# Second MLP product of a hybrid encoder layer: a step of the weight split done by adding or casting DMAs

## Chip, cores and metric

The kernel runs on one core of a Trainium2 chip. The metric is the device time of one execution in microseconds (us).

## What is computed

One layer of a bidirectional encoder on 256 tokens of width 2048 in float32: input projection, attention, a gated linear recurrence, a merge, an MLP, a per-layer embedding and a last norm. The part that the change touches is the second product of the MLP, whose weight `w_down` has 8192 rows and 2048 columns:

```python
h = rmsnorm(x, g_mlp[i])
u = jnp.square(jax.nn.relu(jnp.einsum('bsd,df->bsf', h, w_up[i])))
x = x + jnp.einsum('bsf,fd->bsd', u, w_down[i])
```

## The kernel before

All weights are streamed from HBM once, in chunks of 1 MB: a tile `raw` of 128 partitions by 2048 float32. `load` (L101 to L106) issues one DMA for a chunk on SyncE's queue. The matrix products run in the 32-bit format float32r, whose mantissa is shorter than float32's, and the lost precision is brought back by splitting each operand in two: `hi` is the value rounded to float32r, `lo` the rest. `prep_half` (L108 to L116) does this for half a chunk, 128x1024: ScalarE copies `raw` into a `hi` tile (L112, the copy rounds), VectorE writes `lo` = `raw` - `hi` (L113). `raw` has 3 buffers, `hi` and `lo` have 4 halves each, which is two chunks.

A product is then the sum of three: `x_hi w_hi + x_lo w_hi + x_hi w_lo`. In `gemm_mov` (the second MLP product among others) one chunk holds four blocks of the contraction for 512 columns. TensorE runs 16 matmuls that read the chunk's `hi` halves and then 8 that read its `lo` halves (L196), each 128x512. Blocks 0 and 1 lie in the first half of the chunk, blocks 2 and 3 in the second:

```python
for a, ws in ((0, w[0]), (1, w[0]), (0, w[1])):
    for kk in range(4):
        for t in ts:
            last_mm[0] = pe.matmul(ps[t], xs(X, k)[:, a, t * P:(t + 1) * P], wsl(ws, kk, 512), ...)
```

The order of the chunks is written out in a list at the start (`order`, `plan`). The MLP's steps are u0 u1 d0 u2 d1 u3 d2 d3: a step u computes a quarter of the 8192 hidden features with `w_up` (16 chunks), a step d, here called a pass, multiplies that quarter by `w_down` (16 chunks: four groups j of 512 output columns with four chunks c each), keyed `("dn", 4 * pass + j, c)`. At the end of each group VectorE adds the two accumulators to the residual (L674).

When TensorE's code comes to chunk i, `next_w` (L123 to L132) has issued the loads up to chunk i + 2 and the split of chunk i + 1. A tile framework puts the semaphores: a load waits until the reader of the `raw` buffer's earlier chunk is done, a `hi` or `lo` write until TensorE has read that buffer's earlier half, two chunks back. Each engine, GpSimd (POOL) and SyncE's queue (SP) too, takes its instructions strictly in its own order. POOL computes small things (L300 and others) and issues no DMA.

Of the kernel before, what the change touches and what calls it, by code (L numbers as in the profile page):

```python
# [7 lines left out]
AF = mybir.ActivationFunctionType  # L8
ALU = mybir.AluOpType
AX = mybir.AxisListType  # L10
PSUM = bass.MemoryType.PSUM

P = 128
D = 2048
S = 256
# [11 lines left out]
def build(tc, xT, xtok, pT, gains, gfin_in, ropet, ident_in, masks_in, ghg_in, lb_in,  # L27
          w_mov, w_st, w_oa, w_oh, w_out, w_up, w_dn, w_pg, w_ple, out):
    nc = tc.nc
    act, dve, pool, pe, sp = nc.scalar, nc.vector, nc.gpsimd, nc.tensor, nc.sync  # L30
# [5 lines left out]
    order = []  # L36
# [18 lines left out]
    for step in MLP:  # L55
        c = int(step[1])
# [6 lines left out]
    for j in range(4):  # L63
        plan("pg", 4, j)
    aps = {"in": w_mov, "st": w_st, "oa": w_oa, "oh": w_oh, "out": w_out, "up": w_up, "dn": w_dn, "pg": w_pg,
           "ple": w_ple}

    import contextlib
    with contextlib.ExitStack() as es:
# [14 lines left out]
        def nm(s):  # L84
            cnt[0] += 1
            return f"{s}_{cnt[0]}"
# [7 lines left out]
        def mps():  # L94
            return psm.tile([P, 512], F32, tag="m", name=nm("m"))

# [1 line left out]
        raws, preps = {}, {}  # L98
        pos = [0, 0, 0]

# [7 lines left out]
        def prep_half(i, hf):  # L108
            sl = raws[i][:, hf * 1024:(hf + 1) * 1024]
            hi = wraw.tile([P, 1024], F32R, tag="hi", bufs=4, name=nm("hi"))  # L110
            lo = wraw.tile([P, 1024], F32R, tag="lo", bufs=4, name=nm("lo"))
            act.activation(hi, sl, AF.Copy)  # L112
            dve.tensor_tensor(lo, sl, hi, ALU.subtract)  # L113
            his, los = preps.setdefault(i, ([], []))
            his.append(hi)
            los.append(lo)  # L116
# [14 lines left out]
            pos[0] += 1  # L131
            return preps.pop(i)  # L132

# [1 line left out]
        clock = [0.0]  # L135
        last_mm = [None]
        woven = []
# [24 lines left out]
            o = (k % per) * n  # L162
            return t[:, o:o + n]

        # act tensors are pairs of [P, 8, 2, 256] (hi | lo)
        def xs(X, k):
            return X[k // 8][:, k % 8]

        def gemm_st(key, X, last=None):
            """[128 e, hi-lo x S] in PSUM; `last` runs before the last quarter of the contraction is read."""  # L170
            his, los = next_w(key)
            ps = gps()
            for k in range(KT):
                if k == 12 and last:
                    last()
                x = xs(X, k)
                pe.matmul(ps, wsl(his, k, P), x, start=k == 0, stop=False)  # L177
                pe.matmul(ps[:, :S], wsl(los, k, P), x[:, 0, :], start=False, stop=k == KT - 1)  # L178
                tick(0.327)
            return ps  # L180
# [4 lines left out]
            return z  # L185

        def gemm_mov(arr, j, X, last=None, stagger=False):
            """[128 tokens, 512 e] in PSUM for both token tiles; staggered, the first one ends well before the second."""
            ps = [gps() for _ in range(NT)]

            def chunk(c, w, ts):
                for a, ws in ((0, w[0]), (1, w[0]), (0, w[1])):
                    for kk in range(4):
                        k = 4 * c + kk
                        for t in ts:
                            last_mm[0] = pe.matmul(ps[t], xs(X, k)[:, a, t * P:(t + 1) * P], wsl(ws, kk, 512),  # L196
                                                   start=k == 0 and a == 0 and ws is w[0],
                                                   stop=k == KT - 1 and ws is w[1])
                        tick(0.216 * len(ts))

            for c in range(2 if stagger else 4):
                if c == 3 and last:
                    last()
                chunk(c, next_w((arr, j, c)), range(NT))
            if stagger:
                if last:
                    last()
                ws = [next_w((arr, j, c)) for c in (2, 3)]
                for t in range(NT):
                    for c in (2, 3):  # L210
                        chunk(c, ws[c - 2], (t,))
            return ps
# [2 lines left out]
            return gemm_mov("in", GROUPS.index(g), X)  # L215

        def to_T(srcs, X, e0, gain=None):
            """four [tokens, 128] blocks of both token tiles, transposed, scaled and split into X[e0:e0 + 4]."""
            yield 2.5
            for e in (e0, e0 + 2):  # L220
                tp = mps()
                for a in range(2):
                    for t in range(NT):
                        o = (e - e0 + a) * P
                        pe.transpose(tp[:, a * S + t * P:a * S + (t + 1) * P], srcs[t][:, o:o + P], ident)  # L225
                if gain is None:
                    dst = X[e // 8][:, e % 8:e % 8 + 2]
                    tv = tp.rearrange("p (e t) -> p e t", e=2)
                    act.activation(dst[:, :, 0, :], tv, AF.Copy)
                    dve.tensor_tensor(dst[:, :, 1, :], tv, dst[:, :, 0, :], ALU.subtract)  # L230
                else:
                    for a in range(2):
                        dst, tv, g = xs(X, e + a), tp[:, a * S:(a + 1) * S], gain[:, e + a:e + a + 1]
                        act.activation(dst[:, 0, :], tv, AF.Copy, scale=g)
                        dve.scalar_tensor_tensor(dst[:, 1, :], tv, g, dst[:, 0, :], ALU.mult, ALU.subtract)  # L235
                yield 0.5
# [2 lines left out]
            n = nm("c")  # L239
            return cst.tile(shape, dt, tag=n, name=n)  # L240

# [1 line left out]
        ph1, st1 = open_pool("ph1", side="right")  # L243

        def t1(shape, tag, bufs=1, dt=F32):
# [14 lines left out]
        quarter = lambda X, qd: X[qd // 2][:, 4 * (qd % 2):4 * (qd % 2) + 4]  # L260
# [39 lines left out]
            pool.tensor_tensor(outt, v, nhalf[:, :n], ALU.pow)  # L300

        def bcast_r(rt, R):
            """R [P, S] = rt laid along the free axis on every partition."""
            ps = mps()
            for t in range(NT):
                pe.matmul(ps[:, t * P:(t + 1) * P], rt[:, t:t + 1].to_broadcast([P, P]), ident,
                          start=True, stop=True)
            dve.tensor_copy(R, ps[:, :S])
# [14 lines left out]
        def setup():  # L323
# [12 lines left out]
            dve.tensor_scalar(rtok, rtok, 1.0 / D, EPS, ALU.mult, ALU.add)  # L336
            rsq(rtok, rtok, NT)
            dve.tensor_scalar(rtok_s, rtok, HD ** -0.5, None, ALU.mult)
            # rope tables with the gains folded in: [q|k][cos|sin]
            for w in (1, 0):  # L340
                for t in range(NT):
                    for a in range(2):
# [7 lines left out]
            for qd in range(4):  # L350
# [1 line left out]
                pool.tensor_tensor(xq, xq, R0.unsqueeze(1).to_broadcast([P, 4, S]), ALU.mult)  # L352
                split(Hm, xq, qd)
                yield 3.0
            # hgrn lower bounds: softmax over the two layers, entry 0
            dve.tensor_tensor(lmx, lbt[:, 0], lbt[:, 1], ALU.max)
            dve.tensor_tensor(lex, lbt, lmx.unsqueeze(1).to_broadcast([P, 2, 2, KT]), ALU.subtract)
            act.activation(lex, lex, AF.Exp)
# [2 lines left out]
            dve.tensor_tensor(low, lex[:, 0], lsum, ALU.mult)  # L361
            dve.tensor_tensor(oml, lex[:, 1], lsum, ALU.mult)

# [1 line left out]
        def heads_T(ps, w, tag, pause):  # L365
            """per-head rmsnorm, gain, rope, then transpose into [P(d), 4, hi-lo, S]."""
            zas = []
            for t in range(NT):
                ss = t1([P, 4], "ss", 2)
                scr = t1([P, HD], "scr", 2)  # L370
                for h in range(4):
                    act.activation(scr, ps[t][:, h * HD:(h + 1) * HD], AF.Square,
                                   scale=rtok_s[:, t:t + 1], accum_out=ss[:, h:h + 1])
# [18 lines left out]
            for t in range(NT):  # L392
# [4 lines left out]
                hi, lo = (dstT[:, :, a, t * P:(t + 1) * P] for a in range(2))  # L397
# [76 lines left out]
        flush()  # L474
        st1.close()

# [1 line left out]
        ph2, st2 = open_pool("ph2", side="right")  # L478

        def t2(shape, tag, bufs=2, dt=F32):  # L480
# [4 lines left out]
        def scan_head(h, q, T, vi, gg):  # L485
# [8 lines left out]
            tiles = lambda ap: ap[:, :S].rearrange("p (t s) -> p t s", t=NT)  # L494
# [11 lines left out]
            for li, L in enumerate(LEVELS):  # L506
# [14 lines left out]
                if L < 64:  # L521
# [3 lines left out]
                    T = Tn  # L525
# [5 lines left out]
                    dve.copy_predicated(SD, masks[:, 0].unsqueeze(1).to_broadcast([P, NT, P]), tiles(pd))  # L531
                yield {1: 3.5, 64: 2.6}.get(L, 2.0)
            px = mps()
            # column block t of SX: S^T[s in the other tile, t]
            pe.matmul(px[:, P:2 * P], KK[:, 0, 0:P], QQ[:, 1, P:2 * P], start=True, stop=True)
            pe.matmul(px[:, 0:P], KK[:, 1, P:2 * P], QQ[:, 0, 0:P], start=True, stop=True)
            SX = t2([P, NT, P], "SX", 1)
# [25 lines left out]
        for j in range(4):  # L563
# [11 lines left out]
            for h in range(4 * j, 4 * j + 4):  # L575
                ps = gemm_st(("st", 3 * h), Hm)
                q = t2([P, S], "q")
# [4 lines left out]
                T = t2([P, 2, S], "T1")  # L582
# [4 lines left out]
                    dve.tensor_scalar(T[:, d], T[:, d], oml[:, d, h:h + 1], low[:, d, h:h + 1], ALU.mult, ALU.add)  # L587
                weave(scan_head(h, q, T, vi, gg))

# [1 line left out]
        ctok = lambda tag: [com.tile([P, 512], F32, tag=tag, bufs=2, name=nm(tag)) for _ in range(NT)]  # L591
        MX = None
        for j in range(4):
# [18 lines left out]
                dve.tensor_tensor(ya[t], ya[t], yb[t], ALU.add)  # L612
            weave(to_T(ya, MX, 4 * j))

# [1 line left out]
        xr = bigt(F32, [P, NT, D])  # L616
        for t in range(NT):
            sp.dma_start(xr[:, t], xtok[t])
# [3 lines left out]
        rr = [ctile([P, NT]) for _ in range(3)]  # L622
# [2 lines left out]
            act.activation(junk(), rows(j)[t], AF.Square, accum_out=sums[i][:, t, j:j + 1])  # L625

        def row_r(i, ts=slice(0, NT)):
            """rr[i] = rsqrt(mean square + eps) per token."""
            r = rr[i][:, ts]
            dve.tensor_reduce(r, sums[i][:, ts], AX.X, ALU.add)  # L630
            dve.tensor_scalar(r, r, 1.0 / D, EPS, ALU.mult, ALU.add)  # L631
            rsq(r, r, ts.stop - ts.start)
# [6 lines left out]
                squares(0, j, t)  # L639
            weave(to_T(rows(j), H1, 4 * j, gn[:, 1]))  # L640

# [1 line left out]
        UA = UB = Hp = t4 = None  # L643
        r1s = ctile([P, NT])
        for step in MLP:
            c = int(step[1])
# [30 lines left out]
                if c == 3:  # L677
                    weave(to_T(rows(j), Hp, 4 * j, gn[:, 2]))

# [1 line left out]
        pH = bigt(F32R, [P, 2, 2, S])  # L681
        pf = com.tile([P, 2, S], F32, tag="ya", bufs=2, name=nm("pf"))
        gfin = bigt(F32, [P, D])
# [42 lines left out]


def _stationary(w, n):
    """[2048, 128 n] -> [n, 128 p, 16 k * 128 e]."""
    return np.ascontiguousarray(w.reshape(KT, P, n, P).transpose(2, 1, 0, 3).reshape(n, P, D))  # L730


def _moving(w):
    """[2048, 512 n] -> [n, 4 c, 128 p, 4 k * 512]."""
    return np.ascontiguousarray(w.reshape(4, 4, P, -1, 512).transpose(3, 0, 2, 1, 4).reshape(-1, 4, P, D))


def _feat(v):
    """[..., 2048] -> [128 p, ..., 16 k]."""
    return np.moveaxis(v.reshape(v.shape[:-1] + (KT, P)), -1, 0)  # L740


# [73 lines left out]
```

## Time and profile of the kernel before

| | us |
|---|---|
| median of 2 runs | 1992.3 |
| lowest and highest run | 1992.04, 1992.57 |
| profiled execution, span from first to last instruction | 1992.7 |
| TensorE matmul busy in that span | 1967.5 |
| VectorE busy | 1238.1 |
| ScalarE busy | 947.6 |
| GpSimd busy | 144.0 |

The profile is of one execution, read by the hardware profiler; the page gives its span and no other time for it, and this span is 0.4 us longer than the median of the timed runs. A row of the timeline begins with its start and its length in us. `x16` behind a row is the count of instructions that were merged into it. PE is TensorE, DVE VectorE, ACT ScalarE, SPq SyncE's DMA queue. A matmul's length counts its way through the array, so matmuls overlap, and the distance of starts is what one costs.

### The profile page before, as it was taken

How to read it: one execution, taken by the hardware profiler on the slowest of the kernel's cores; microseconds unless marked ns; L12 is line 12 of the kernel's file. 1: busy time of each engine (PE TensorE's matmuls, PEld its weight loads, DVE VectorE, ACT ScalarE, POOL GpSimd, SP SyncE). 2: the span in 40 equal slices, each digit the busy share in tenths (PEclk: the TensorE clock that was granted, in tenths of full speed). 3: DMA queues.
4: the chain of work that ended last, by engine and by line, in shares of the span. 5: the costliest groups of instructions: out<-in, count | busy, mean ns of one | idle time of the engine just before them, and what ended most of it. 6: DMA issues, size and time to landing. Idle time of an engine off the chain costs nothing.

```text
span 1992.7 us, 25647 instructions
## 1 busy us (share of the span) xinstructions
PE 1967.5 (99%) x9948; PEld 1664.1 (84%) x9948; DVE 1238.1 (62%) x1722; ACT 947.6 (48%) x1495; POOL 144.0 (7%) x175
## 2 busy tenths in 40 slices
PE   8999999999999999999999999999999999999998
PEld 6788888888888888888888888888888888888886
DVE  6877687686785874545545566665565456545555
ACT  5576555454554553444443454443344344434543
POOL 2300030120220210000000000000000000000001
PEclk9999999999999999999999999999999999999999
DMA  8444444544434435555565555555555555555553
GB/s 324 167 145 148 148 149 148 175 142 166 166 136 168 167 138 183 189 194 186 192 240 192 183 175 186 189 190 190 190 190 190 190 185 189 197 190 181 201 193 123
DMA packets 51673, 358.56 MB, mean 180 GB/s; under 512 B 5984, under 2 KB 6240, under 8 KB 9056
## 3 DMA queue, kind: packets, MB, share of 16 engines
q1 hardware_dynamic: 51552, 356.93, 50.7%
q8 instruction: 78, 1.28, 0.2%
q14 instruction: 43, 0.35, 0.0%
HBM read 354.81 MB, written 2.10 MB: 179 GB/s over the span
## 4 chain that ended last, share of the span: by engine, by line
PE 96%; DVE 2%; issue 1%; DMA 1%; ACT 0%; POOL 0%; SPq 0%; POOLq 0%; DVEq 0%; ACTq 0%
PE g L196 58%; PE g L177 20%; PE g L178 10%; PE m L509 3%; PE m L443 1%; PE m L423 1%; PE g L696 1%; DMA big<-xT 1%; DVE lo L113 1%; PE m L225 1%; PE m L544 0%; PE m L529 0%; PE m L543 0%; PE m L454 0%; ACT hi L112 0%
## 5 line engine op out<-in xcount | busy, mean ns | idle before, releaser
L113 DVE TENSOR_TENSOR lo<-raw,hi 128x1024 fp32r<-128x1024 f32 x660 | 810.2, 1246 | 649.4 <-ACT hi L112 593.0
L112 ACT ACTIVATE hi<-raw 128x1024 fp32r<-128x1024 f32 x660 | 679.0, 1055 | 807.0 <-PE g L196 488.6
L196 PE MATMUL g<-hi,big 128*128 128x512 f32 x2688 | 658.8, 394 | 9.0 <-ACT hi L112 9.0
L177 PE MATMUL g<-big,hi 128*128 128x512 f32 x1792 | 643.9, 402 | 0.0
L196 PEld LDWEIGHTS g<-hi,big 128*128 128x128 f32 x2688 | 501.8, 189 | 111.2 <-ACT hi L112 10.3
L178 PE MATMUL g<-big,lo 128*128 128x256 f32 x1792 | 503.3, 281 | 0.0
L177 PEld LDWEIGHTS g<-big,hi 128*128 128x128 f32 x1792 | 337.3, 188 | 76.5 <-DVE big L235 0.3
L196 PE MATMUL g<-lo,big 128*128 128x512 f32 x1344 | 344.2, 394 | 0.0
L178 PEld LDWEIGHTS g<-big,lo 128*128 128x128 f32 x1792 | 340.0, 190 | 0.4
L196 PEld LDWEIGHTS g<-lo,big 128*128 128x128 f32 x1344 | 249.3, 189 | 49.0
L196 PE MATMUL g<-hi,UB 128*128 128x512 f32 x512 | 125.1, 396 | 0.0
L196 PEld LDWEIGHTS g<-hi,UB 128*128 128x128 f32 x512 | 96.2, 188 | 22.4
L300 POOL TENSOR_TENSOR c<-c,c 128x2 f32<-128x2 f32 (+1 forms) x5 | 3.2, 640 | 1164.2 <-DVE c L631 1150.5
L509 PE MATMUL m<-QQ,kc 128*128 128x128 f32 x448 | 72.8, 286 | 2.8 <-ACT kc L501 2.6
L509 PEld LDWEIGHTS m<-QQ,kc 128*128 128x128 f32 x448 | 64.1, 191 | 11.5 <-ACT kc L501 5.3
L501 ACT ACTIVATE kc<-KK 128x256 f32<-128x256 f32 x112 | 47.7, 436 | 50.8 <-PE m L509 25.9
L523 POOL TENSOR_TENSOR T<-T 128x256 f32<-128x256 f32 (+2 forms) x96 | 54.0, 563 | 202.6 <-DVE T L587 186.7
L196 PE MATMUL g<-lo,UB 128*128 128x512 f32 x256 | 65.5, 396 | 0.0
L196 PE MATMUL g<-hi,MX 128*128 128x512 f32 x256 | 63.3, 397 | 0.0
L516 DVE TENSOR_TENSOR QQ<-QQ,T 128x256 f32<-128x256 f32 x112 | 52.2, 466 | 13.0 <-PE m L509 13.0
L513 DVE TENSOR_TENSOR KK<-KK,T 128x256 f32<-128x256 f32 x112 | 54.8, 492 | 5.5 <-ACT kc L501 2.6
L196 PEld LDWEIGHTS g<-lo,UB 128*128 128x128 f32 x256 | 48.0, 188 | 11.0
(145 smaller groups left out, 1101.5 us busy)
## 6 DMA issues: line engine op xcount, KB each, us to landing
raw<-w_mov SPq DMA_DIRECT2D x87, 1024.0 KB, 4.8
raw<-w_up SPq DMA_DIRECT2D x64, 1024.0 KB, 4.8
raw<-w_dn SPq DMA_DIRECT2D x64, 1024.0 KB, 4.8
raw<-w_st SPq DMA_DIRECT2D x48, 1024.0 KB, 4.8
raw<-w_oa SPq DMA_DIRECT2D x16, 1024.0 KB, 4.8
raw<-w_oh SPq DMA_DIRECT2D x16, 1024.0 KB, 4.8
raw<-w_out SPq DMA_DIRECT2D x16, 1024.0 KB, 4.8
raw<-w_pg SPq DMA_DIRECT2D x16, 1024.0 KB, 4.8
```

The source lines that it names most:

```text
L112: act.activation(hi, sl, AF.Copy)
L113: dve.tensor_tensor(lo, sl, hi, ALU.subtract)
L177: pe.matmul(ps, wsl(his, k, P), x, start=k == 0, stop=False)
L178: pe.matmul(ps[:, :S], wsl(los, k, P), x[:, 0, :], start=False, stop=k == KT - 1)
L196: last_mm[0] = pe.matmul(ps[t], xs(X, k)[:, a, t * P:(t + 1) * P], wsl(ws, kk, 512), start=k == 0 and a == 0 and ws is w[0], stop=k == KT ...
L225: pe.transpose(tp[:, a * S + t * P:a * S + (t + 1) * P], srcs[t][:, o:o + P], ident)
L423: pe.matmul(sc[:, t * S:(t + 1) * S], qT[:, i, a, t * P:(t + 1) * P], kT[:, j, b], start=n == 0, stop=n == 2)
L501: act.activation(kc.rearrange("p (n a b) -> p n a b", a=2, b=L), merged(KK, 0, L, S // (2 * L)), AF.Copy)
L509: pe.matmul(pl[:, t * P:(t + 1) * P], kc[:, t * P:(t + 1) * P], merged(QQ, t * P, L, P // (2 * L)), start=True, stop=True)
L513: dve.tensor_tensor(kv, kv, view(T, 1, [[2, nb // 2], [nb - 1, 2], [0, L]]), ALU.mult)
L516: dve.tensor_tensor(qv, qv, view(T, nb + 1, [[2, nb // 2], [-(nb + 1), 2], [0, L]]), ALU.mult)
L523: pool.tensor_tensor(Tn, view(T, 0, [[nb, 2], [2, nb // 2]]), view(T, 1, [[nb, 2], [2, nb // 2]]), ALU.mult)
```

## The change

In passes d0, d1 and d2, for the chunks c = 1 and c = 3 of every group (here called odd chunks), one step of the split is given to a DMA that GpSimd issues. There are 8 such chunks or 16 halves in each pass, 48 halves in all.

- d0 ("hbm"): VectorE's subtraction is gone. ScalarE writes `lo` = -`raw`, rounded to float32r as `hi` is, and a DMA adds the half chunk, read a second time from HBM, to `lo`.
- d1 ("sbuf"): the same, but the DMA's source is the `raw` tile in SBUF.
- d2 ("cast"): ScalarE's copy is gone. A DMA reads the half chunk a second time from HBM and casts it into `hi`. VectorE's subtraction stays.

Pass d3, the even chunks and all other weights are as before. The comments of the file are taken out too, and lines below the new code are numbered 10 higher.

```diff
         def prep_half(i, hf):
             sl = raws[i][:, hf * 1024:(hf + 1) * 1024]
             hi = wraw.tile([P, 1024], F32R, tag="hi", bufs=4, name=nm("hi"))
             lo = wraw.tile([P, 1024], F32R, tag="lo", bufs=4, name=nm("lo"))
-            act.activation(hi, sl, AF.Copy)
-            dve.tensor_tensor(lo, sl, hi, ALU.subtract)
+            key = order[i]
+            how = ("hbm", "sbuf", "cast", None)[key[1] // 4] if key[0] == "dn" and key[2] % 2 else None
+            src = aps[key[0]][key[1:]][:, hf * 1024:(hf + 1) * 1024]
+            if how == "cast":
+                pool.dma_start(hi, src)
+            else:
+                act.activation(hi, sl, AF.Copy)
+            if how in ("hbm", "sbuf"):
+                act.activation(lo, sl, AF.Copy, scale=-1.0)
+                pool.dma_start(lo, src if how == "hbm" else sl, accum_op=ALU.add)
+            else:
+                dve.tensor_tensor(lo, sl, hi, ALU.subtract)
```

What this makes of the engines' orders is shown at three places. ScalarE's order in pass d0, from the chunk c = 2 of the first group on (tiles `raw_2127`), then the odd chunk c = 3 (`raw_2132`) and the next even one; before:

```order
L112 ACTIVATE hi_2133_11561<-raw_2127_11525 128x1024
L665 ACTIVATE UB1_1874_9965<-uu_2124_11519 128x256
L112 ACTIVATE hi_2135_11565<-raw_2127_11525 128x1024
L112 ACTIVATE hi_2138_11595<-raw_2132_11559 128x1024
L112 ACTIVATE hi_2140_11599<-raw_2132_11559 128x1024
L112 ACTIVATE hi_2143_11629<-raw_2137_11593 128x1024
```

and in the changed kernel:

```order
L118 ACTIVATE hi_2133_11563<-raw_2127_11525 128x1024
L118 ACTIVATE hi_2135_11567<-raw_2127_11525 128x1024
L118 ACTIVATE hi_2138_11597<-raw_2132_11561 128x1024
L118 ACTIVATE hi_2140_11602<-raw_2132_11561 128x1024
L120 ACTIVATE lo_2139_11598<-raw_2132_11561 128x1024
L120 ACTIVATE lo_2141_11603<-raw_2132_11561 128x1024
L118 ACTIVATE hi_2143_11633<-raw_2137_11595 128x1024
L118 ACTIVATE hi_2145_11637<-raw_2137_11595 128x1024
```

The two new copies of the odd chunk stand behind both of its `hi` copies and ahead of the next chunk's. On VectorE the subtractions of the odd chunks are gone and nothing else changes places but for a row at the ends of the passes. GpSimd's order around the MLP before, where `c_1755` is a small power of the MLP's norm and `c_1756` that of the next norm:

```order
L300 TENSOR_TENSOR c_1755_9245<-c_1755_9245,c_3_78 128x2
L300 TENSOR_TENSOR c_1756_9246<-c_1756_9246,c_3_78 128x2
L712 TENSOR_TENSOR big_1749_9237<-big_1749_9237,big_2751_15437 128x512 x6
L300 TENSOR_TENSOR c_1757_9247<-c_1757_9247,c_3_78 128x1 x2
L812 UNCONDITIONAL_BRANCH
```

and in the changed kernel, where the first of the 48 DMAs follow:

```order
L310 TENSOR_TENSOR c_1755_9245<-c_1755_9245,c_3_78 128x2
L121 DMA lo_2129_11528<-w_dn 128x1024
L121 DMA lo_2131_11533<-w_dn 128x1024
L121 DMA lo_2139_11598<-w_dn 128x1024
L121 DMA lo_2141_11603<-w_dn 128x1024
L121 DMA lo_2151_11672<-w_dn 128x1024
L121 DMA lo_2153_11677<-w_dn 128x1024
```

All 48 stand in a row between the two small powers, with no compute of GpSimd among them. SyncE's queue in pass d1 with what each load waits for, where DVE and Activation are engines, DMASW the DMAs that GpSimd issued and DMAHW SyncE's own; before:

```order
L105 DMA raw_2348_12919<-w_dn 128x2048 [waits DMAHW3_49,DVE_49]
L105 DMA raw_2353_12953<-w_dn 128x2048 [waits DMAHW4_49,DVE_49]
L105 DMA raw_2358_12987<-w_dn 128x2048 [waits DMAHW5_49,DVE_49]
L105 DMA raw_2365_13025<-w_dn 128x2048 [waits DMAHW6_49,DVE_49]
L105 DMA raw_2370_13059<-w_dn 128x2048 [waits DMAHW7_49,DVE_49]
L105 DMA raw_2375_13093<-w_dn 128x2048 [waits DMAHW0_49,DVE_49]
```

and in the changed kernel:

```order
L105 DMA raw_2348_12937<-w_dn 128x2048 [waits DMAHW3_49,DVE_49]
L105 DMA raw_2353_12971<-w_dn 128x2048 [waits DMASW1_49,DMAHW4_49,DMASW0_49,Activation_49]
L105 DMA raw_2358_13007<-w_dn 128x2048 [waits DMAHW5_49,DVE_49]
L105 DMA raw_2365_13045<-w_dn 128x2048 [waits DMASW3_49,DMAHW6_49,DMASW2_49,Activation_49]
L105 DMA raw_2370_13081<-w_dn 128x2048 [waits DMAHW7_49,DVE_49]
L105 DMA raw_2375_13115<-w_dn 128x2048 [waits DMASW5_49,DMAHW0_49,DMASW4_49,Activation_49]
```

Every second load, the one that takes over the buffer of an odd chunk, waits for both adding DMAs of that chunk where it waited for VectorE. The loads behind it wait in line.

## Rows read from the trace of the kernel before

**Rows 1.** The page: span, and part 1 (busy time, share, instructions).
```profile
span 1992.7 us, 25647 instructions
PE 1967.5 (99%) x9948; PEld 1664.1 (84%) x9948; DVE 1238.1 (62%) x1722; ACT 947.6 (48%) x1495; POOL 144.0 (7%) x175
```

**Rows 2.** Busy time by stretch: the four passes of the second product.
```profile
core 0: us, PE busy (x) PEld busy (x) DVE busy (x) ACT busy (x) POOL busy (x), PEclk, DMA share, GB/s
1349.20:1436.30 87.10, 87.10 (x386) 72.18 (x385) 42.55 (x41) 33.77 (x35) 0.00 (x0) 1.00 0.56 196
1526.70:1616.00 89.30, 89.30 (x386) 72.53 (x385) 42.63 (x41) 33.76 (x35) 0.00 (x0) 1.00 0.54 192
1704.70:1791.80 87.10, 87.10 (x386) 72.15 (x385) 42.54 (x41) 33.79 (x35) 0.00 (x0) 1.00 0.57 197
1791.80:1883.90 92.10, 92.10 (x410) 74.63 (x409) 48.67 (x54) 41.68 (x57) 0.00 (x0) 1.00 0.56 195
```

**Rows 3.** The page, part 5: the weight split and the largest matmul group.
```profile
L113 DVE TENSOR_TENSOR lo<-raw,hi 128x1024 fp32r<-128x1024 f32 x660 | 810.2, 1246 | 649.4 <-ACT hi L112 593.0
L112 ACT ACTIVATE hi<-raw 128x1024 fp32r<-128x1024 f32 x660 | 679.0, 1055 | 807.0 <-PE g L196 488.6
L196 PE MATMUL g<-hi,big 128*128 128x512 f32 x2688 | 658.8, 394 | 9.0 <-ACT hi L112 9.0
```

**Rows 4.** Timeline of TensorE in pass d0: start, length, instruction, count.
```profile
1376.29 3.79 PE L196 MATMUL g<-hi,big 128*128 128x512 f32 x16
1379.92 1.98 PE L196 MATMUL g<-lo,big 128*128 128x512 f32 x8
1381.73 3.79 PE L196 MATMUL g<-hi,big 128*128 128x512 f32 x16
1385.36 1.98 PE L196 MATMUL g<-lo,big 128*128 128x512 f32 x8
```

**Rows 5.** Timeline of ScalarE, the same stretch; in brackets the wait before.
```profile
1373.77 2.01 ACT L112 ACTIVATE hi<-raw 128x1024 fp32r<-128x1024 f32 x2 [3.43 <-PE g L196]
1379.21 2.01 ACT L112 ACTIVATE hi<-raw 128x1024 fp32r<-128x1024 f32 x2 [3.43 <-PE g L196]
```

**Rows 6.** Timeline of VectorE, the same stretch.
```profile
1375.64 2.36 DVE L113 TENSOR_TENSOR lo<-raw,hi 128x1024 fp32r<-128x1024 f32 x2 [1.76 <-ACT hi L112]
1381.09 2.36 DVE L113 TENSOR_TENSOR lo<-raw,hi 128x1024 fp32r<-128x1024 f32 x2 [3.08 <-ACT hi L112]
```

**Rows 7.** Timeline of SyncE's queue, the same stretch.
```profile
1378.03 0.33 SPq L105 DMA_DIRECT2D raw<-w_dn  x1
1383.47 0.33 SPq L105 DMA_DIRECT2D raw<-w_dn  x1
```

**Rows 8.** Waits of SyncE's queue in pass d0: total, times, longest.
```profile
SPq L105 <- DVE lo L113: 74.8, 15, 6.4
```

**Rows 9.** Busy time by stretch: one weight load; the full queue at the start.
```profile
1383.00:1384.00 1.00, 1.00 (x6) 0.81 (x5) 0.45 (x1) 0.00 (x0) 0.00 (x0) 1.00 0.00 0
1384.00:1388.00 4.00, 4.00 (x19) 3.34 (x18) 1.48 (x2) 2.01 (x2) 0.00 (x0) 1.00 0.74 262
1388.00:1389.40 1.40, 1.40 (x8) 1.17 (x7) 0.89 (x1) 0.00 (x0) 0.00 (x0) 1.00 0.00 0
22.00:24.00 2.00, 2.00 (x11) 1.65 (x10) 2.00 (x2) 0.00 (x0) 2.00 (x3) 1.00 1.01 422
```

**Rows 10.** DMA issues by line: count, KB each, median us to landing.
```profile
raw<-w_dn SPq DMA_DIRECT2D x64, 1024.0 KB, 4.8
...
big<-xtok SPq DMA_DIRECT2D x4, 512.0 KB, 8.3
big<-xT SPq DMA_DIRECT2D x3, 512.0 KB, 10.7
raw<-w_mov SPq DMA_DIRECT2D x2, 512.0 KB, 5.7
```

**Rows 11.** Line L105 in pass d0: landing of its loads.
```profile
DMA to landing us min/median/max: 4.7/4.8/6.0
```

## The prediction

> **What bounds the kernel now.** I read the page's busy times first: TensorE is busy for 99% of the span, VectorE for 62%, ScalarE for 48%, GpSimd for 7% [rows 1]. A share over the whole span can hide a stage with another limit, so the next view is busy time by stretch, cut at the four passes of the second product: TensorE is busy for the whole of each, at the full granted clock, while VectorE works 43 of 87 us and ScalarE 34 [rows 2]. So nothing that only relieves VectorE or ScalarE can shorten the three passes that change. The largest groups of instructions say what is relieved: a subtraction of VectorE takes 1.25 us, a copy of ScalarE 1.06 us, and TensorE's largest group waited 9.0 us in all for ScalarE [rows 3].
>
> The question is then by how much the weight split runs ahead of TensorE, and for that I read the timeline of one place in d0. A chunk takes 1381.73 - 1376.29 = 5.44 us, 24 matmuls at 0.227: 16 on `hi`, and from 3.63 us on 8 on `lo` [rows 4]. The two `hi` copies at 1373.77 are for the chunk that starts at 1381.73 [rows 4, 5]. ScalarE waited 3.43 us for them, for TensorE: the buffers are those of two chunks back, so this start is as early as the buffers allow. The subtractions of that chunk run from 1375.64 to 1378.00 [rows 6]. The view blames their wait on ScalarE; but in the next chunk the first `hi` copy ends at about 1380.2 and the subtraction begins only at 1381.09, right behind the fourth `lo` matmul of the chunk at 1379.92 [rows 4 to 6]. What comes free last is the `lo` buffer. At 1378.03 SyncE issues the load that takes over the `raw` buffer [rows 7], which it waits for 15 times in the pass [rows 8].
>
> **The change part by part.** VectorE loses 32 subtractions, 32 x 1.246 = 40 us; ScalarE gains 32 copies and loses 16, 16 x 1.055 = 17 us [rows 3]. Both lie beside matmuls: the copies of an odd chunk become four, 4.2 of 10.9 us per pair of chunks, or 6.3 with the even chunk's two. I count both at 0 us. If that cover were gone, ScalarE would be late by the 1.06 us of a copy.
>
> *d0 and d1.* ScalarE's order is two `hi` copies, then two of `lo`. The first `lo` copy starts at 1375.78, where the `hi` copies end (its buffer came free at 1375.64), and ends at 1376.83; the second ends at 1377.89, before the next `hi` copies at 1379.21 [rows 5, 6]. GpSimd can then issue its DMAs at 1376.83 and 1377.89. Behind a waiting DMA on GpSimd stand only further DMAs, and no engine waits for those before their own chunk. TensorE reads the first `lo` half at 1385.36 and the second 4 x 0.227 later, at 1386.27 [rows 4]. The DMAs have 8.5 and 8.4 us.
>
> No row shows an adding DMA, nor any DMA issued by GpSimd. I build its time from loads. A 1 MB load lands after 4.8 us [rows 10]; the one issued at 1383.47 moves between 1384 and 1388, with nothing ahead of it and nothing behind [rows 7, 9]. Where the queue is full, 422 GB/s are moved, so 1.05 MB occupies the DMA engines for 2.5 us [rows 9]; the other 2.3 us are start and landing. An odd chunk's two halves are 1 MB. Let r be the engine time of this DMA against a plain load. One load (issued at 1378.03) moves beside it and may take its 2.5 us first. Both halves have then landed at 1376.83 + 2.3 + 2.5 + 2.5 r = 1381.63 + 2.5 r, against 1386.27. The end is met up to r = 1.86; behind that every odd chunk stalls TensorE for 2.5 r - 4.64 us. Sixteen odd chunks stand in the two passes:
> - r = 1, a plain copy, the low end: 2.1 us to spare, 0 us.
> - r = 1.5 (two reads and a write where a copy has one of each): 0.9 us to spare, 0 us.
> - r = 2 (if reads set the pace): 0.36 us late, 16 x 0.36 = 6 us.
> - r = 3: 2.86 us late, 46 us. This end is from the slowest small loads: 512 KB landed after 8.3 and 10.7 us at the start, where other transfers stood in the queue, against 2.3 + 1.25 = 3.55 us alone by the same sum [rows 10], a factor of 2.3 to 3.
>
> The nearest row is the load itself (r = 1), which in d0 lands within 4.7 to 6.0 us with the engines 0.56 occupied [rows 2, 11], and an add reads once more than that. I take r = 1.75, between 1.5 and 2, and for its price the middle of theirs, 3 us, because landings scatter by up to 1.3 us and the 0.27 us that 1.75 leaves is less.
>
> The Trainium skill ("Collectives: The Full Stack", Part 3, on why ReduceScatter is half as fast as AllGather) says that the add itself costs nothing in a DMA, but that two source reads halve the rate. By that rule r is 2 and the sum is 6 us in place of 3. No row here shows an adding DMA.
>
> In d1 the `raw` buffer of an odd chunk comes free only when its DMAs have landed, at 1381.63 + 2.5 x 1.75 = 1386.0, not at 1378.03. The load behind it lands 4.8 us later at 1390.8, 0.7 us after ScalarE would start on it (1373.77 + 3 x 5.44 = 1390.09), and TensorE needs it at 1381.73 + 16.32 = 1398.05, with 2.0 us of copies before. The next load, queued behind it on SyncE, lands 2.5 us later, before ScalarE's 1395.5. That is 0 us with 5 us of cover; without the cover each microsecond costs 8 us in the pass.
>
> *d2.* The casting DMAs need only the `hi` buffer: issue at 1373.77 and, four matmuls later, 1374.68. With the same sum both halves are there at 1373.77 + 4.8 + 2.5 r = 1378.57 + 2.5 r; TensorE reads the second half at 1381.73 + 0.91 = 1382.64 [rows 4, 5]. r = 1 leaves 1.6 us; r = 2 is 0.93 us late, 8 x 0.93 = 7 us. The subtractions, 2.4 us behind the cast, end before 1386.27 in both cases. A cast moves the same bytes as a load, so I take r = 1: 0 us. New on VectorE is that its subtraction waits for a DMA; behind it in line are the additions of L674, which stand behind an even chunk's pair and so do not wait.
>
> *Sum.* 3 us of stalls in d0 and d1, nothing else. The profiled span of 1992.7 would become 1995.7; the median of the timed runs is 0.4 us lower than that span, so the forecast is 1992.3 + 3 = 1995 us.
>
> The Trainium skill ("DMA: Bandwidth & Descriptors", Specifications) gives a first byte after about 1 us on GpSimd's path and 0.6 us on SyncE's. With 0.4 us more of start the sum at r = 2 would be 16 x 0.76 = 12 us. No row here shows GpSimd's path.
>
> **The rivals.**
> - *Late landing, a few microseconds.* r lies between 1.9 and 2.8, or GpSimd takes 1 to 2 us more to start a DMA than SyncE. The price runs from 16 x 0.1 to 16 x 2.4 us: 1994 to 2030, at its middle 2012 us. For it: the margin at r = 1.75 is only 0.3 us. Against: with two queues beside each other the load need not go first, as I let it.
> - *The DMA engines are too slow with an add, and the kernel becomes slower.* Place: the `lo` halves of the 16 odd chunks in d0 and d1; TensorE waits before its 17th matmul or 21st. At r = 3.5 each waits 4.1 us, 66 us, 2058 us. It decides (2% is 40 us, 2.5 us per odd chunk) from r = 2.86. For it: the small loads at the start took three times their sum [rows 10], and the engines' share is already 0.56. Against: those stood behind several MB, and here 5.0 + 2.5 r us of engine time fit into a pair of chunks (10.88 us) up to r = 2.35.
> - *Faster.* The relief of VectorE would have to reach TensorE. In d0 to d2 TensorE has no idle time to give back [rows 2], and in the whole span it has 25 us [rows 1], less than 2%. Price: 0 to -2 us.
> - *The DMAs do not do in hardware what their names say* and move as plain copies: r = 1, 1992 us.
>
> **How the numbers follow.** The forecast (no stall, or under 0.4 us per odd chunk) has 0.54, late landing 0.19, slow adds 0.25, faster 0.01, plain copies 0.01. A measurement of this kernel tells about 2% from no change. Faster by that is 0.01, slower 0.25, the rest 0.74. The range begins at 1990, just below no change, and ends at adds with r = 3 and casts with r = 2, 1992.3 + 46 + 7 = 2045; above that I leave some 0.17.
>
> **What would show it right or wrong.** Right: three passes without idle time of TensorE, 5.44 us per chunk, adding DMAs that land within 8.4 us of the copies' end, casts within 8 us of the issue. Wrong: TensorE waits before the `lo` matmuls of odd chunks (slow adds), before their `hi` matmuls (slow casts), or in d1 alone for a late load. d3 must stay as it is; if it grows, the cause is not in the DMAs. A GpSimd queue on which one issue takes more than 4 us would break the sum at its first step.

## The result, and the profile after

The changed kernel takes 2039.6 us (two runs, 2039.2 to 2040.0) against 1992.3: a ratio of 1.0232, 95% interval 1.0214 to 1.0249, so slower by 2.3%. That lies inside the range of 1990 to 2045, but the forecast said 1995 us and gave "within 2%" a chance of 0.74.

The page of the changed kernel, for [rows 1], and its part 5, for [rows 3] (every line of the changed kernel stands 10 further down than before, so L118 is the `hi` copy, L123 the subtraction and L206 the matmul):

```profile
span 2037.4 us, 25743 instructions
...
PE 1982.2 (97%) x9948; PEld 1665.3 (82%) x9948; DVE 1201.5 (59%) x1690; ACT 964.1 (47%) x1511; POOL 180.9 (9%) x223
...
q0 software_dynamic: 6912, 25.17, 5.7%
...
L123 DVE TENSOR_TENSOR lo<-raw,hi 128x1024 fp32r<-128x1024 f32 x628 | 771.6, 1248 | 692.4 <-ACT hi L118 476.1
L118 ACT ACTIVATE hi<-raw 128x1024 fp32r<-128x1024 f32 x644 | 662.5, 1055 | 802.7 <-PE g L206 447.8
L206 PE MATMUL g<-hi,big 128*128 128x512 f32 x2688 | 666.3, 396 | 18.7 <-ACT hi L118 9.9
```

VectorE lost 32 subtractions and some 37 us of work, ScalarE gained 16.5 us, as counted; a new queue, q0, moved 25.17 MB for the 48 half DMAs. None of this is where the time went; the idle time before the `hi` matmuls, 18.7 us where it was 9.0, is a first sign of it. Busy time by stretch, the passes d0, d1, d2 and d3, for [rows 2] (columns as there):

```profile
1346.90:1453.40 106.50, 94.51 (x385) 74.71 (x385) 25.63 (x26) 48.98 (x50) 14.10 (x16) 0.95 0.91 240
1543.90:1648.60 104.70, 96.29 (x387) 74.85 (x386) 25.65 (x27) 48.84 (x50) 13.83 (x16) 0.95 0.85 225
1737.40:1836.40 99.00, 90.25 (x386) 71.18 (x386) 43.76 (x42) 18.78 (x20) 8.08 (x15) 1.00 0.68 245
1836.40:1928.50 92.10, 92.10 (x410) 74.55 (x409) 48.66 (x54) 41.69 (x57) 0.00 (x0) 1.00 0.58 208
```

From the first matmul of a pass to that of the next segment, d0 grew from 87.1 to 106.6 us (19.5), d1 from 89.2 to 104.7 (15.5) and d2 by 11.9; d3 is what it was, at 92.1. The three sum to 46.9; the span grew by 44.7, because the up-projection ahead of d0, whose code did not change, took 3.2 us less in this execution (it takes either 178.6 to 178.7 or 181.9 us in every trace of this case, whatever the change, so single executions differ by about 3 us). The granted clock fell to 0.95 in d0 and d1: with 0.95 x 106.5 = 101.2 us of full clock, some 5.3 us of d0 and, likewise, 5.2 us of d1 are clock. What is left, 14.2 and 10.3 us there and 11.9 in d2, goes with waiting. TensorE's waits (for whom, us in total, times, longest), where the only row of this line before the change was that for ScalarE, of 9.0 us:

```profile
PE g L206 <- DMA lo<-w_dn: 11.9, 7, 2.6
PE g L206 <- ACT hi L118: 9.9, 3, 7.3
PE g L206 <- DMA hi<-w_dn: 8.8, 10, 1.6
PE g L206 <- DMA lo<-raw: 8.4, 9, 1.4
```

Three of the four rows are the three kinds of new DMA: adds from HBM (d0), casts (d2), adds from the `raw` tile (d1). They hold 11.9 of the 14.2 us in d0, 8.4 of 10.3 in d1 and 8.8 of 11.9 in d2; the other 2 to 3 us of each pass stand in no row of matmul waits and were not taken apart.

One such place in d0: TensorE's timeline, then GpSimd's and SyncE's queue.

```profile
1376.81 1.98 PE L206 MATMUL g<-lo,big 128*128 128x512 f32 x8
1378.63 3.79 PE L206 MATMUL g<-hi,big 128*128 128x512 f32 x16
1383.62 1.20 PE L206 MATMUL g<-lo,big 128*128 128x512 f32 x4 [1.20 <-DMA lo<-w_dn]
1387.39 1.41 PE L206 MATMUL g<-lo,big 128*128 128x512 f32 x4 [2.58 <-DMA lo<-w_dn]
1388.60 5.23 PE L206 MATMUL g<-hi,big 128*128 128x512 f32 x16
```

```profile
1373.92 1.81 POOL L121 DMA_DIRECT2D lo<-w_dn  x2 [10.85 <-ACT lo L120]
```

```profile
1374.60 6.10 SPq L105 DMA_DIRECT2D raw<-w_dn  x2
```

The two adds went out one behind the other from 1373.92 and the second, issued some 0.9 us after the first, had landed only at 1387.39, where TensorE wanted it at 1384.81. SyncE issued a load at 1374.60 and another at 1380.37 (6.10 us from the first's start to the second's end). The stretches of that wait:

```profile
1377.00:1387.00 10.00, 6.61 (x28) 4.81 (x27) 2.36 (x2) 4.17 (x5) 0.80 (x1) 1.00 1.02 304
1387.00:1388.00 1.00, 0.61 (x3) 0.52 (x4) 0.00 (x0) 0.00 (x0) 0.07 (x1) 1.00 0.74 82
1388.00:1389.00 1.00, 1.00 (x4) 0.79 (x3) 0.00 (x0) 0.16 (x1) 0.00 (x0) 0.60 0.64 49
1389.00:1390.00 1.00, 1.00 (x4) 0.79 (x3) 0.00 (x0) 0.89 (x1) 0.00 (x0) 0.50 0.82 139
```

For ten microseconds the 16 DMA engines were occupied throughout (share 1.02): 3.0 of the 3.1 MB of two loads and one chunk's adds, at 304 GB/s where loads alone make 422 [rows 9]. Of the same ten microseconds the loads' queue q1 and the adds' queue q0 have (packets, MB, share of the 16 engines):

```profile
q1 hardware_dynamic: 272, 2.06, 52.7%
q0 software_dynamic: 265, 0.95, 48.6%
```

That is 5.3 us for 2.06 MB and 4.9 us for 0.95 MB, or 2.6 us and 5.1 us per MB: the adds take twice what a load of their size takes. And right behind the wait the granted clock falls, to 0.60 in the mean of one microsecond and then to 0.50, the lower level of 1.2 GHz: sixteen matmuls take 5.23 us instead of 3.79. The next odd chunk does not wait; its second add, issued at 1390.19 behind this stall, landed after 8.4 us instead of 12.5. The long waits fall on about every second odd chunk.

In d1 the clock fell three times too, and no wait there is longer than 1.4 us. Each time it fell behind two waits in one chunk, here the first time, with the stretch that follows:

```profile
1577.01 1.20 PE L206 MATMUL g<-lo,UB 128*128 128x512 f32 x4 [1.37 <-DMA lo<-raw]
1579.45 2.07 PE L206 MATMUL g<-lo,UB 128*128 128x512 f32 x4 [1.24 <-DMA lo<-raw]
```

```profile
1579.40:1582.80 3.40, 3.35 (x8) 2.68 (x9) 0.00 (x0) 1.06 (x1) 0.87 (x1) 0.51 0.67 183
```

### The profile page after: what moved, and what is told of

Read it like the earlier page. It is cut to its first block, busy times and chain, and to the rows that moved or that the text cites. A ratio compares the mean times of both kernels' runs of the same rounds, so it can differ in the third digit from the quotient of the medians.

```text
span 2037.4 us, 25743 instructions
## 1 busy us (share of the span) xinstructions
PE 1982.2 (97%) x9948; PEld 1665.3 (82%) x9948; DVE 1201.5 (59%) x1690; ACT 964.1 (47%) x1511; POOL 180.9 (9%) x223
## 3 DMA queue, kind: packets, MB, share of 16 engines
q0 software_dynamic: 6912, 25.17, 5.7%
q8 instruction: 78, 1.28, 0.2%
## 4 chain that ended last, share of the span: by engine, by line
PE 82%; DMA 10%; issue 4%; DVE 2%; ACT 1%; POOL 0%; SPq 0%; POOLq 0%; DVEq 0%; ACTq 0%
PE g L206 47%; PE g L187 19%; PE g L188 10%; DMA lo<-raw 4%; DMA hi<-w_dn 3%; DMA lo<-w_dn 3%; PE m L519 3%; DVE lo L123 1%; PE m L453 1%; PE m L433 1%; PE g L706 1%; PE m L235 1%; ACT lo L120 0%; ACT hi L118 0%; PE m L554 0%
## 5 line engine op out<-in xcount | busy, mean ns | idle before, releaser
L123 DVE TENSOR_TENSOR lo<-raw,hi 128x1024 fp32r<-128x1024 f32 x628 | 771.6, 1248 | 692.4 <-ACT hi L118 476.1
L118 ACT ACTIVATE hi<-raw 128x1024 fp32r<-128x1024 f32 x644 | 662.5, 1055 | 802.7 <-PE g L206 447.8
L206 PE MATMUL g<-hi,big 128*128 128x512 f32 x2688 | 666.3, 396 | 18.7 <-ACT hi L118 9.9
L206 PEld LDWEIGHTS g<-hi,big 128*128 128x128 f32 x2688 | 503.9, 190 | 127.0 <-DMA hi<-w_dn 13.4
L206 PE MATMUL g<-lo,big 128*128 128x512 f32 x1344 | 346.4, 394 | 12.0 <-DMA lo<-w_dn 11.9
L206 PEld LDWEIGHTS g<-lo,big 128*128 128x128 f32 x1344 | 248.4, 188 | 64.5 <-DMA lo<-w_dn 16.0
L206 PE MATMUL g<-hi,UB 128*128 128x512 f32 x512 | 127.4, 400 | 0.0
L206 PEld LDWEIGHTS g<-hi,UB 128*128 128x128 f32 x512 | 98.1, 192 | 23.5
L206 PE MATMUL g<-lo,UB 128*128 128x512 f32 x256 | 69.8, 410 | 8.4 <-DMA lo<-raw 8.4
L206 PEld LDWEIGHTS g<-lo,UB 128*128 128x128 f32 x256 | 48.4, 193 | 23.0 <-DMA lo<-raw 12.3
L206 PE MATMUL g<-hi,MX 128*128 128x512 f32 x256 | 63.3, 396 | 0.0
L206 PEld LDWEIGHTS g<-hi,MX 128*128 128x128 f32 x256 | 47.8, 188 | 11.3
```

## The experiments

The first four runs were set against two theories of the late halves. S: GpSimd's queue starts a DMA some 2 us later than a load's queue. E: an add occupies the DMA engines twice as long as a copy. The third was timed ten times, the others once. Beside the first four the kernel before took 1991.5 us (median of 13 runs, 1990.8 to 1997.7), beside the last three 1992.4 (one run).

**Half the bytes.** Only the first half of each 1024 columns is added or cast by DMA. In d0 and d1 the other 512 columns of `lo` get no add, so that half of the add is left out.

```
-                pool.dma_start(hi, src)
+                act.activation(hi[:, 512:], sl[:, 512:], AF.Copy)
+                pool.dma_start(hi[:, :512], src[:, :512])
...
-                pool.dma_start(lo, src if how == "hbm" else sl, accum_op=ALU.add)
+                pool.dma_start(lo[:, :512], (src if how == "hbm" else sl)[:, :512], accum_op=ALU.add)
```

> The DMAs of the odd chunks move only the first 512 of 1024 columns, 256 KB in place of 512 KB; the other half of each lo tile keeps -raw in d0 and d1 (the add is left out there), and in d2 ScalarE copies the other half of hi. Theory S (start): a DMA that GpSimd issues has about 2 us more of fixed time between issue and landing than a load of SyncE (4.2 against 2.3 us), so the shortest landing falls only from 6.2 to about 5.2 us in d0 and from 5.5 to about 4.9 in d2, and d0 and d2 keep 2 to 6 us of their growth of 19.5 and 11.9 us. Theory E (engines): the landing is engine time, twice that of a load with an add; the shortest landing falls to about 3.9 us in d0, and all three passes go back to within 2 us of 87.1, 89.2 and 87.1 us.

Measured: 1997.4 us; d0 90.1, d1 89.2 (as before the change), d2 92.0, 4.9 us longer than before. The 256 KB adds of d1 landed after 3.3 to 5.3 us:

```profile
DMA to landing us min/median/max: 3.3/3.9/5.3
```

Those of d0 landed after 4.2 us at the least and 7.1 in the median (6.2 and 9.2 in the changed kernel), the casts of d2 after 3.6 and 7.8 (5.5 and 8.2). A fixed extra start of 2 us on top of the 2.3 us of a load would leave nothing for moving in the shortest of each pass, so S has no room, and the shortest one of d0 is near E's 3.9. But E's other sign, all passes within 2 us of before, is there in d1 alone: d0 keeps 3.0 us and d2 4.9. Casts of half the size land hardly earlier in the median, so their own bytes are not what makes them late; E says nothing of what moves beside them.

**Plain copies.** The same bytes at the same times as copies without add or cast, into a scratch tile; VectorE subtracts as before. d0 copies from HBM and d1 from `raw` on GpSimd's queue, d2 from HBM on ScalarE's queue.

```
-            how = ("hbm", "sbuf", "cast", None)[key[1] // 4] if key[0] == "dn" and key[2] % 2 else None
+            how = ("hbm", "sbuf", "act", None)[key[1] // 4] if key[0] == "dn" and key[2] % 2 else None
...
+                act.activation(sc, sl, AF.Copy, scale=-1.0)
+                (act if how == "act" else pool).dma_start(sc, sl if how == "sbuf" else src)
+                sl = sc
```

> No add and no cast: in odd chunks a plain DMA copies the weight into a scratch tile (which ScalarE has written first, so that the issue comes at the same time as in the changed kernel), and VectorE subtracts from that. d0: GpSimd issues, source HBM. d1: GpSimd issues, source the raw tile. d2: ScalarE's queue issues, source HBM. Theory S: GpSimd's plain copies land after at least 5.4 us and in the median about 8, d0 and d1 grow by about 10 us each (the subtraction comes on top); those of ScalarE's queue land after at least 3.6 and in the median under 6 us, and d2 grows by at most 3 us. Theory E: without the add all three land alike, 3.6 us at least and 5 to 6 in the median, and no pass grows by more than 3 us.

Measured: 1997.4 us; d0 90.2, d1 89.2, d2 no longer than before. The 512 KB copies on GpSimd's queue, from HBM:

```profile
sc<-w_dn POOLq DMA_DIRECT2D x14, 512.0 KB, 4.5
```

and those on ScalarE's queue:

```profile
sc<-w_dn ACTq DMA_DIRECT2D x14, 512.0 KB, 4.0
```

GpSimd's path costs 0.5 us, not 2. Without the add the loss all but vanishes (E had allowed 3 us, d0 keeps 3.1): adds are needed for it. (The Trainium skill's figures in "DMA: Bandwidth & Descriptors", Specifications, differ by 0.4 us between the two paths; this pair of rows, taken in different passes, agrees.)

**One chunk more of lead.** The same adds and casts, issued a chunk earlier, with one more pair of half tiles for every second odd chunk.

```
...
+            while pos[3] < pos[1]:
+                if pos[3] >= pos[2]:
+                    ahead(pos[3])
+                pos[3] += 1
```

> All adds and casts stay, but each is issued one chunk (5.4 us) earlier, with one more pair of half buffers: 13 to 14 us from issue to use in place of 8. If latency is all (theory S), the three passes go back to 87, 89 and 87 us and the time to 1992 to 1996 us. If the engines are too slow for the bytes (theory E): in the changed kernel's d0 an adding half took 3.2 us of the 16 engines (47.7% of 100 us over 15 halves) and a load 2.9, so a pair of chunks needs 2 x 3.2 + 2 x 2.9 = 12.2 of 10.9 us, and d0 stays 8 to 10 us longer, d1 (2.66 us per half) about 2 us, d2 none: about 2003 us.

Measured over ten runs: 1996.6 us, ratio 1.0016 (1.0005 to 1.0027), so no change that 2% could tell. Pass d0:

```profile
1349.00:1437.00 88.00, 87.61 (x387) 72.07 (x386) 24.41 (x25) 47.48 (x49) 12.20 (x14) 1.00 1.00 288
```

The DMA engines are occupied throughout (share 1.00) and adds land later than ever (medians 10.6 and 11.1 us for the two kinds of tile in d0, against 9.2), yet TensorE waits 0.4 us in all for these DMAs and its clock stays at 1.00. So the engines' throughput, which theory E had expected to cost 8 to 10 us in d0, does not bind; what cost the time is the stretch from issue to use.

**A fourth raw buffer in d1**, so that a `raw` tile held by a late add delays no load.

```
+            if key[0] == "dn" and key[1] // 4 == 1 and key[2] == 1:
+                r = extra[0]([P, 2048], "raw4", 1)
...
```

> The changed kernel with a fourth raw buffer in d1, where every other odd chunk's tile gets a buffer of its own, so that loads wait less for the adding DMAs. If d1's growth of 15.5 us comes from the landing of the DMAs alone, d1 stays at 102 to 105 us. If late loads carry a good part of it (ScalarE waited 23.9 us for loads in d1 of the changed kernel), d1 falls to 99 us or less. d0 and d2 stay at 106 and 99 us under both.

Measured: 2041.7 us, d1 104.6 against 104.7. ScalarE's wait for loads in d1 (23.9 us in the changed kernel) is gone, and the pass is not shorter: the late release of `raw` does not set the pass's length, as the prediction had it. But the 104.6 us are made up otherwise: TensorE waited 11.1 us for adds where it was 8.4, and the clock fell once where it was three times. Two waits in one chunk, nearly as long as those shown above for d1, left it at 1.00 here:

```profile
1618.45 1.20 PE L209 MATMUL g<-lo,UB 128*128 128x512 f32 x4 [1.18 <-DMA lo<-raw]
1620.92 1.19 PE L209 MATMUL g<-lo,UB 128*128 128x512 f32 x4 [1.28 <-DMA lo<-raw]
```

```profile
1618.00:1632.00 14.00, 11.69 (x48) 8.88 (x48) 3.77 (x4) 5.99 (x7) 1.74 (x2) 1.00 0.82 223
```

That left open why adds of twice the engine time made every second odd chunk 3 to 4 us late, how much of the loss was clock, and why casts were late. The next three were for these.

**Filling the gap.** Eight matmuls into a spare accumulator ahead of the second `lo` half of odd chunks in d0 and d1.

```
+                        if fill and kk == 2 and ws is w[1]:
+                            sp_ = mps()
+                            for f in range(8):
+                                pe.matmul(sp_, xs(X, k)[:, 0, :P], wsl(w[0], 0, 512), start=True, stop=True)
```

> Eight matmuls into a spare accumulator are put ahead of the second lo half of every odd chunk of d0 and d1, some 1.8 us of extra TensorE work in each of 16 chunks (28.8 us in all) just where the late half is waited for; the output stays the same. Theory C: the clock falls because TensorE stood idle for more than 2 us, so with the gap filled the mean granted clock of d0 and d1 goes from 0.95 back to 0.99 or more, and as the fill takes the place of the longest waits d0 takes 102 to 106 us and d1 101 to 105 (105 and 103.5 if the fill costs 14.4 a pass and what is left of the waits about 3). Rival: the clock falls for another cause (the DMA load, say); then it stays at 0.95, some 5 us a pass are lost as before, and d0 takes 108 to 112 us, d1 107 to 110.

Measured: passes of 102.8 and 104.1 us with 14.5 us more work in each (64 matmuls at 0.227); the whole 2043.8 us, of which d2, not edited, has 3.2 us more than in the changed kernel. d0 and d1:

```profile
1350.80:1453.60 102.80, 102.10 (x451) 83.99 (x450) 25.69 (x27) 48.91 (x50) 14.08 (x16) 1.00 0.94 249
...
1544.00:1648.10 104.10, 104.10 (x450) 84.47 (x449) 25.63 (x27) 48.65 (x50) 13.85 (x16) 1.00 0.85 245
```

The DMAs and their load are the same, the clock is 1.00: the fall of the clock hung on TensorE standing idle. That it takes more than 2 us of idling, as theory C has it, is not what the traces show: in d1 of the changed kernel it fell behind waits of 1.4 us and less, and a wait of 2.24 us late in d0 of the last run below left it at 1.00. How much idling it takes stays open. d0 with the extra work is even 3.8 us shorter than with waits.

**Half the loads.** In d0 to d2 the even chunks reuse the `raw` tile of the odd chunk before (the first of a pass loads); loading and using the even chunks' own weights is left out.

```
+            if key[0] == "dn" and key[1] < 12 and key[2] % 2 == 0 and (key[1] % 4 or key[2]):
+                raws[i] = raws[i - 1]
+                return
```

> In d0, d1 and d2 the even chunks reuse the raw tile of the odd chunk before them instead of loading their own (the first chunk of a pass still loads): the weights of the even chunks are left out, half of the loads of these passes are gone, and no load moves while the half DMAs of an odd chunk do, or one at most. Theory L: an adding DMA takes about 2.1 times the engine time of a load of its size, and what makes the halves late is that two loads, not one, move beside them. Both halves then land 2.1 x 2.5 = 5.3 us of engine time after the issue plus 2.3 fixed, for the second half 7 to 8.5 us where it was 12.5; no wait is over 0.5 us, d0 takes 87 to 89 us, d1 89 to 91, d2 87 to 88, the span 1994 to 2000. Rival F: an adding or casting DMA is late by itself (a fixed time or a rate that doesn't depend on neighbours); then the second half still lands after 11 us or more, and d0 stays above 98, d1 above 98 and d2 above 94.

Measured: 2010.1 us; d0 92.3, d1 89.2, d2 93.1. In d1 the growth of 15.5 us is gone, and the adds landed after 4.6 to 7.7 us:

```profile
DMA to landing us min/median/max: 4.6/5.5/7.7
```

In d0 5.2 us of 19.5 are left, with landings of 6.1 to 11.2 us; the longest wait, 2.5 us, is in its last chunk, beside two loads of the next product, which the edit did not touch. That is between L and F in d0 and d2, and L alone in d1; all three passes stay below what F asks for. This run also shows the add by itself, a load alone and then one chunk's adds alone in d1:

```profile
1545.00:1546.50 1.50, 1.50 (x8) 1.24 (x7) 0.00 (x0) 1.50 (x2) 0.40 (x1) 1.00 1.02 421
1547.50:1552.50 5.00, 5.00 (x23) 4.08 (x22) 2.21 (x2) 2.01 (x2) 0.41 (x1) 1.00 1.06 202
```

With all engines occupied in both, 421 GB/s against 202: r = 2.1, for a source in SBUF. Adds from HBM without a load beside them, in d0 of this run, come to 2.2:

```profile
1367.00:1370.00 3.00, 3.00 (x15) 2.50 (x14) 2.36 (x2) 0.53 (x1) 0.00 (x0) 1.00 1.02 193
```

In d2 a load still went out beside each pair of casts (issue of the second cast at 1768.90, of the load at 1769.14), and the second half was up to 2.0 us late.

**Casts with the raw tile released early.** In d2 VectorE subtracts from a copy that ScalarE makes, so that `raw` does not wait for the cast.

```
                 pool.dma_start(hi, src)
+                sc = extra[0]([P, 1024], "sc")
+                act.activation(sc, sl, AF.Copy)
+                sl = sc
```

> In d2 ScalarE copies each half of the raw tile into a scratch tile and VectorE subtracts from that, so that the raw buffer comes free when ScalarE has read it, as before the change, and not when the cast has landed. d0 and d1 are untouched (106 and 105 us). Theory B: the raw tiles come free in pairs in d2, SyncE's loads go out in pairs and two of them share the engines with a cast; with the loads spread again the second cast lands within 7 us and d2 takes 87 to 90 us instead of 99, the span 2026 to 2029. Rival: the cast is late by itself (its rate is half that of a load, or its start is late); then d2 stays at 96 to 99 us and the span at 2035 to 2039.

Measured: 2034.9 us; d2 90.1 us, and the casts land after 5.3 us (median) instead of 8.2:

```profile
1741.90:1832.00 90.10, 88.22 (x386) 71.75 (x385) 43.71 (x42) 32.05 (x34) 8.08 (x15) 1.00 0.74 264
```

That is theory B's number for the pass, but not its picture: the loads still go out in pairs, the latest cast landed after 8.9 us and not within 7, and the span of 2033.1 us lies between B's and the rival's, as d0 took 107.5 us and the up-projection ahead of it 181.9. What moved is the loads' place. First the casts and loads of the changed kernel, GpSimd and then SyncE:

```profile
1757.95 0.54 POOL L116 DMA_DIRECT2D hi<-w_dn  x1 [10.50 <-PE g L206]
1758.86 0.54 POOL L116 DMA_DIRECT2D hi<-w_dn  x1 [0.37 <-PE g L206]
...
1756.88 2.60 SPq L105 DMA_DIRECT2D raw<-w_dn  x2
```

then this run's:

```profile
1762.75 0.54 POOL L116 DMA_DIRECT2D hi<-w_dn  x1 [9.22 <-PE g L209]
1763.66 0.54 POOL L116 DMA_DIRECT2D hi<-w_dn  x1 [0.37 <-PE g L209]
...
1764.97 0.83 SPq L105 DMA_DIRECT2D raw<-w_dn  x2
```

In the changed kernel the pair of loads went out around the casts, the first 1.1 us ahead of them; here it follows the second by 1.3 us. The cast's own rate is not what made it late.

## Why the forecast was wrong and the range held

- *Engines and what bounds* (right). VectorE's relief and ScalarE's copies cost and gave nothing, and TensorE's time decides. The late release of `raw` does not lengthen d1, as the run with a fourth buffer shows.
- *The engine time of an add* (mis-sized). The step "I take r = 1.75, between 1.5 and 2" failed: it is 2.1 to 2.2 (202 and 193 against 421 GB/s). The rule of the Trainium skill ("Collectives: The Full Stack", Part 3), that two source reads halve the rate, says 2, and here the trace agrees, for adds from HBM and from SBUF. By the prediction's own formula r = 2.1 is 0.6 us per odd chunk, 10 us instead of 3. The 2.5 us of a load were short too: the load by itself in [rows 9] has a share of 0.74 over 4.00 us, which is 3.0 us.
- *What moves beside it* (the step that failed most). "One load (issued at 1378.03) moves beside it and may take its 2.5 us first": it was two. Adds that have not landed when SyncE issues its next load, here 5.8 us after the one before, share the engines with that one too. With 2.5 us more, the formula gives 3.1 us per late odd chunk; the one shown above waited 1.20 + 2.58 = 3.8 us and then the next not at all. In all waiting held d0 and d1 up by 14.2 + 10.3 us. With half the loads gone, d1 lost nothing and d0 5.2 us; with copies in place of adds and all loads there, d1 nothing and d0 3. It takes both.
- *The clock* (not in the sum). About 10.5 us of d0 and d1 are lost by matmuls at the lower clock. It fell three times in d0, behind single waits of 2.6 us, and three times in d1, behind two waits in one chunk that came to 1.7 to 2.6 us; in d2, where the longest wait was 1.6 us, it stayed at 1.00, and with the gaps filled it did so in d0 and d1 too. Waits of 2.5 us in a chunk of d1 in the fourth run (1.18 + 1.28) and of 2.6 in one of d0 in the last (0.32 + 2.24) were not followed by a fall, so the sum of a chunk's waits does not settle it.
- *The casts* (wrong by 12 us). r = 1 was not the fault: the step was "the same sum", 4.8 + 2.5 r, in which one load of 2.5 us goes first and then the cast. VectorE's subtraction, which waits for the cast, now releases `raw`, so SyncE's loads go out in pairs and at the casts' own time: 3.1 MB, 7.5 us of engine time, where 5.0 were counted. By the same sum the second load makes each odd chunk 0.9 us late, 7 us in the pass; the other 5 were not taken apart. The prediction looked at who waits behind that subtraction on VectorE, and not at the buffer that it sets free. Released early, the pass costs 3 us instead of 12.
- *Sum.* By an estimate with the prediction's formula 3 became 10 by r, and 14 more, the rest of 24.5, go to the second load; no run parts the two. 10.5 came from the clock and 12 from d2, together 47, less about 2 us by which the code around the passes ran shorter: 44.7 on the span.
- *The range* (held in part by luck). Its upper end added 46 us for adds with r = 3 and 7 for casts with r = 2. No row or run shows either r; as large a time came from an r of 2, a second load and the clock, and the last two stood in no term.
- *Rivals.* The slower one had the right place (the `lo` halves of odd chunks) and the right sign, but asked for r of 2.86; late landing had the right r (1.9 to 2.8) and too low a price, 2030 us at most. The point against the slower one, that the engines' time fits into a pair of chunks up to r = 2.35, was true and of no use: throughput did not bind, the time from issue to use did. That the issue on GpSimd is short (0.54 us a cast, 0.9 an add) and d3 unchanged came as said.

Open: the 3 us by which d0 stays longer with half the bytes and with plain copies, and the rest of 5.2 us in d0 and 6 us in d2 with half the loads, were not taken apart further than the waits named above.

## What to carry to other kernels

Give a DMA that takes over a step on the way to the matmul the lead of its worst neighbourhood: its own bytes, times two if it adds (2.1 to 2.2 here), plus every transfer that can start before it has landed, and check which buffer its consumer releases, since that sets when the next transfers start. A share of DMA time well under 1 does not tell that it will be in time (d2 lost 12 us at 0.68), and a share of 1.00 does not tell that it will be late (d0 with one chunk more of lead); the lead does. Where TensorE had never idled, count its waits at more than their length, because matmuls behind them may run at half the clock: here 10.5 us came on top of 24.5.

## What the runs showed of the hardware

- A DMA that adds moved 202 GB/s (source in SBUF) or 193 (in HBM) with all engines occupied, where loads moved 421 to 422; one of 512 KB that only copies landed after 4.5 us on GpSimd's queue and 4.0 on ScalarE's.
- After a wait of 2.6 us the granted clock was 0.60, 0.50 and 0.50 in the next three microseconds (0.69 in the fourth), and 16 matmuls took 5.23 us for 3.79. It also fell behind two waits of 1.37 and 1.24 us with four matmuls between them, and did not behind 1.18 and 1.28. With eight matmuls of no use in each gap it stayed at 1.00.
- With one load beside it, a 512 KB cast landed 9.8 us after its issue, although little moved in its last 3 us. Half the loads, d2, the end of that transfer:

```profile
1775.00:1776.00 1.00, 1.00 (x6) 0.83 (x5) 0.00 (x0) 0.18 (x1) 0.00 (x0) 1.00 0.39 152
1776.00:1777.00 1.00, 0.76 (x4) 0.30 (x2) 0.00 (x0) 0.00 (x0) 0.00 (x0) 1.00 0.18 70
1777.00:1778.00 1.00, 0.00 (x0) 0.00 (x0) 0.00 (x0) 0.00 (x0) 0.00 (x0) 1.00 0.06 25
```

A share of 0.18 and then 0.06 is, in the mean, three engines of 16 and then one. This reads as a landing set by the slowest engines, up to 3 us behind the others; the view does not name them, and why they lag was not tried.
